# Seven-product up-projection: partial sums added in PSUM banks instead of by VectorE

## The chip, the cores and the metric

The kernel runs on one core of a Trainium2 chip. The metric is the device time of one execution in microseconds (us). Before the change the median of three runs is 2451.78 us (2449.66 to 2457.12).

## The reference

One layer of a hybrid backbone on 2048 latent tokens of width 1024: a token mixer (gated recurrence and gMLP), its output projection, then a gated MLP with a 3x3 depthwise convolution. The change lies in the MLP's first half. Cut to that:

```python
GRID_W = 64; D_FF = 2816
h2 = modulate(rmsnorm(x, norm_ffn), sh2, sc2)          # x: (1, 2048, 1024)
a, g = jnp.split(h2 @ w_up, 2, axis=-1)                # w_up: (1024, 2 * 2816)
g = g.reshape(1, 32, 64, 2816)                         # 32 rows of the grid, 64 wide
gc = depthwise_conv_3x3(g, taps, 'SAME') + conv_b
x = x + g2 * ((a * gelu(gc)) @ w_down)
```

All of it is fp32.

## The kernel before, in words

Every fp32 product is made of three matmuls: an operand is split into a high half in the fast fp32r form (a ScalarE cast) and a low half (the rest, a GpSimd subtraction, in function `split`, lines 131 and 132), and the sum of high x high, high x low and low x high goes into one PSUM bank (`mm3`, line 65 by way of the class `Tensor`).

The up-projection saves multiplications by a Strassen-Winograd scheme with seven products for a two-by-two block product. One **unit** is two channel tiles of 128 channels (f and f+1) by one half of the sequence (`hh`, 1024 tokens). It has a kind: `"g"`, the gate branch that is convolved, or `"a"`, the value branch that is multiplied with the GELU. There are 44 units, 22 in each half of the sequence, and 308 products. A product i has K = 512, four steps of 128, with three 128x512 matmuls each: 12 matmuls into one bank. The scheme's sums of weights (`Unit.prep`) are made by GpSimd, three products ahead of use (`LOOK = 3`); four buffers each hold the high (`Ah`) and low (`Al`) weight tiles. The token side, seven high and seven low tiles `B`, was made before and lies in SBUF.

The list `prods` sets the order: units go in pairs, and the products of the two units of a pair alternate, with the second unit three places behind:

```python
at = first[n] if n < 2 else [14 * (n // 2) + 2 * i + 3 * (n % 2) for i in range(7)]
```

In the middle of each half, a pair is one `"g"` unit and the `"a"` unit of two channel pairs earlier, which by then has its convolved gate; the first pair is `"g"`, `"g"` and the last `"a"`, `"a"`.

Each product gets a bank of its own from `ubank` (four banks in turn). `after(u, i, p)` takes it out. Product 0 is copied to an SBUF tile `keep` by ScalarE (line 1454); products 2 and 3 are added to it by VectorE (1457, 1460); product 4 serves twice, once in a result and once in the running sum (1472 or 1480); products 1, 4, 5 and 6 each end a quarter of the unit's result, by a VectorE addition into the gate tile `gp` (1466), or, for the value branch, by an addition and a multiplication into the tile `cv` (1473 and 1474 on VectorE, or 1476 on VectorE and 1477 on GpSimd).

When a gate unit is done, `conv` runs for each of its two channel tiles as a generator: two of its steps are called behind each product. ScalarE writes the first tap and the bias into two PSUM banks (tag `dn`, line 1382), VectorE adds eight taps (1385), and ScalarE takes the GELU out into `cv` (1399 in the first half, 1404 in the second). The two halves of the sequence share a row border. The first half leaves the last row's unfinished sum in DRAM, and the second half loads it into an SBUF tile `edges` (1373, 1374), adds the three missing taps there (1390, VectorE), takes the GELU (1405, ScalarE) and multiplies it with the value row left by the first half (1406, GpSimd). `put_m` stores finished tiles.

At the start of the stage the last two token tiles of the step before (the second norm, lines 1239 to 1267) are still in work, spread between the first products by `bg_q.slot()`.

A list scheduler that works from estimated durations orders the instructions of each engine when the kernel is built, except where `pin` keeps the program's order. Each engine then runs its list strictly in that order.

Of the kernel before, what the change touches and what calls it, by code (L numbers as in the profile page):

```python
# [9 lines left out]
F32 = mybir.dt.float32  # L10
# [3 lines left out]
AF = mybir.ActivationFunctionType  # L14
ALU = mybir.AluOpType
# [3 lines left out]
P = 128  # L19
# [9 lines left out]
NF = FF // P  # L29
GW = 64  # L30
# [53 lines left out]
def tile_trunk(ctx, tc, x, c, cx, c_ctx, w_ada, b_ada, norm_mix, norm_ffn, w_in, hg_norm, sgu_g, sgu_b,  # L84
               w_sp, b_sp, w_out, w_up, conv_w, conv_b, w_down, norm_final, masks, out):
    nc = tc.nc
    V, S, G, T = nc.vector, nc.scalar, nc.gpsimd, Tensor(nc.tensor)
# [1059 lines left out]
    xah = pb.tile([P, NR, 4, 512], F32R, tag="xah", name="xah", align_bytes=AL)  # L1147
    xal = pb.tile([P, NR - 1, 4, 512], F32R, tag="xal", name="xal", align_bytes=AL)

    def ubank():  # L1150
        return ps2.tile([P, 512], F32, tag="up", name="up", bufs=4)

    def dbank():
        return ps2.tile([P, 2, 512], F32, tag="dn", name="dn", bufs=2)
# [55 lines left out]
        order += [("a", NF // 2 - 2), ("a", NF // 2 - 1)]  # L1210
        units += [Unit(hh, *o, (1, 2) if n % 2 else (3, 0)) for n, o in enumerate(order)]
    prods = []
    first = [(0, 1, 2, 4, 8, 10, 12), (3, 5, 6, 7, 9, 11, 13)]
    for n, u in enumerate(units):
        at = first[n] if n < 2 else [14 * (n // 2) + 2 * i + 3 * (n % 2) for i in range(7)]
        prods += [(at[i], u, i) for i in range(7)]
    prods = [(u, i) for _, u, i in sorted(prods, key=lambda t: t[0])]
    LOOK = 3
    raw_at = {}
# [138 lines left out]
    def g_rows(hh, f, n2):  # L1358

        return view(gp[f % 4], (1 + 2 * n2) * RW + 1, [[4 * RW, 4], [RW, 2], [1, GW]])  # L1360
# [16 lines left out]
    def conv(hh, f, e):  # L1377

        gt = gp[f % 4]
        cp = dbank().rearrange("p a b -> p (a b)")  # L1380
        cr = cp.rearrange("p (r c) -> p r c", c=GW)
        S.activation(cr, gt[:, 0:RH, 0:GW], AF.Identity, bias=cvb[:, f:f + 1], scale=taps[:, f:f + 1])  # L1382
        yield
        for t in range(1, 9):
            V.scalar_tensor_tensor(out=cr, in0=gt[:, t // 3:t // 3 + RH, t % 3:t % 3 + GW],  # L1385
                                   scalar=taps[:, t * NF + f:t * NF + f + 1], in1=cr, op0=ALU.mult, op1=ALU.add)
            yield
        if hh:
            for t in range(6, 9):
                V.scalar_tensor_tensor(out=e[:, 0, :], in0=gt[:, 1, t % 3:t % 3 + GW],  # L1390
                                       scalar=taps[:, t * NF + f:t * NF + f + 1], in1=e[:, 0, :],
                                       op0=ALU.mult, op1=ALU.add)
        tapped.add((hh, f))
        while out_v[0] == 3:
            yield "full"
        out_v[0] += 1
        vt = v_tile()
        if hh == 0:
            pin(S.activation(vt[:, :TH - GW], cp[:, :TH - GW], AF.Gelu))
            S.copy(e[:, 0, :], cp[:, TH - GW:])  # L1400
            S.dma_start(gs_d[f][:, 1, :], e[:, 0, :])
            pin(G.memset(vt[:, TH - GW:TH], 1.0))
        else:
            pin(S.activation(vt[:, GW:], cp, AF.Gelu))  # L1404
            S.activation(e[:, 0, :], e[:, 0, :], AF.Gelu)
            pin(G.tensor_mul(vt[:, :GW], e[:, 0, :], e[:, 1, :]))
        vals[hh, f] = vt
        yield
# [36 lines left out]
    def quad(p, kind):  # L1445
        return p.rearrange("p (j c) -> p j c", c=P) if kind == "a" else p.rearrange("p (j r c) -> p j r c", r=2, c=GW)

    def after(u, i, p):

        hh, f, kind = u.hh, u.f, u.kind  # L1450
        if i == 0:
            t = pf.tile([P, 2 * 512], F32, tag="keep", name="keep", bufs=2)
            u.u, u.u3 = t[:, :512], t[:, 512:]
            S.copy(u.u, p)
            return
        if i == 2:
            V.tensor_add(u.u, p, u.u)
            return
        if i == 3:
            V.tensor_add(u.u3, p, u.u)  # L1460
            return
        c, n2, add = {1: (0, 0, u.u), 4: (1, 1, u.u3), 5: (0, 1, u.u3), 6: (1, 0, u.u)}[i]
        if kind == "g":
            if f >= 4:
                need(tapped, (hh, f + c - 4))
            V.tensor_add(g_rows(hh, f + c, n2), quad(p, kind), quad(add, kind))  # L1466
        else:
            need(vals, (hh, f + c))
            o = v_cols(hh, f + c, n2)
            if i < 5:  # L1470
                if i == 4:
                    V.tensor_add(u.u, p, u.u)
                V.tensor_add(p, p, add)
                V.tensor_mul(o, quad(p, kind), o)
            else:
                V.tensor_add(add, p, add)  # L1476
                G.tensor_mul(o, quad(add, kind), o)
                put_m(hh, f + c)
        if kind == "g" and i == 4:
            V.tensor_add(u.u, p, u.u)  # L1480
        if kind == "g" and i == 6:
            for ff in (f, f + 1):
                if hh == 0:
                    st(gs_d[ff][:, 0, :], gp[ff % 4][:, RH, 1:GW + 1])
                else:
                    ld(gp[ff % 4][:, 0, 1:GW + 1], gs_d[ff][:, 0, :])
                work.append(conv(hh, ff, edge(hh, ff)))
# [33 lines left out]
    for n, (u, i) in enumerate(((2, 4), (2, 6), (1, 4))):  # L1521
# [2 lines left out]
            ld(t, a_src(0, 0, n))  # L1524
            early[n] = t
        raw_at[pos[len(units) - u, i]] = load
    assert max(n for n, (u, i) in enumerate(prods) if i < NR) == NP - 6
    for n, (u, i) in enumerate(prods):
        now[0] = n
        while stores and (stores[0][0] <= n):  # L1530
            stores.pop(0)[1]()
        while back and back[0] <= n:
            back.pop(0)
            out_v[0] -= 1
        p = ubank()
        hi, lo = u.A[i]
        for k in range(4):
            mm3(p, hi[:, k, :], lo[:, k, :], B[i][0][:, k, :], B[i][1][:, k, :], k == 0, k == 3)
            bg_q.slot()
        if n == 11:  # L1540
            bg_q.drain()
        if n == 12:
            edges = px.tile([P, 7, P], F32R, tag="yst", name="edges", bufs=2, align_bytes=AL).bitcast(F32)
            edges = edges[:, :4, :].rearrange("p f (w c) -> p f w c", w=2)
        with tc.issue_after(scaled[-1].ins) if n < 8 else nullcontext():
            after(u, i, p)
        for j in range(7):
            if last_use[j] == n - 4:
                for w in range(2):
                    load_b(1, j, w)  # L1550
        prep(n + LOOK)
# [266 lines left out]
```

## Time and profile before

| | |
|---|---|
| median of three runs | 2451.78 us |
| profiled execution | 2450.25 us, span 2448.4 us |
| granted clock | 0.997 |
| busy: TensorE / VectorE / ScalarE / GpSimd | 99% / 73% / 39% / 36% |
| first and last matmul of the up-projection start | 1171.3 and 2020.0 us |

PE is TensorE, PEld its weight loads, DVE VectorE, ACT ScalarE, POOL GpSimd, SP SyncE (which issues most DMAs). L1385 is line 1385 of the kernel. In the rows of groups the busy time comes first, then the mean duration of one instruction in ns, then the time that the engine sat idle just before the group and what ended that idle time. In rows of a timeline the first number is the start in us from the span's start, the second the duration. A row of waits gives the total, the number of times and the longest. Matmuls overlap one another in the records (389 ns each), so their pace is read from how many start in a stretch.

### The profile page before, as it was taken

What the parts mean: (1) busy time and instruction counts of PE and PEld (TensorE: products, weight loads), DVE (VectorE), ACT (ScalarE), POOL (GpSimd) and SP (SyncE); (2) the same over time, 40 slices, a digit from 0 to 9 for tenths busy, and PEclk for the clock granted to TensorE, in tenths of its full rate; (3) what the DMA queues carried; (4) which work ended last, traced back from release to release, by engine and by line L of the source; (5) the groups of instructions that cost most, each with busy time, mean ns of one, the idle gap of its engine ahead of it and who ended that gap; (6) DMA issues with size and microseconds to landing.
All of it is one profiled execution on the core that took longest, in us unless ns stands there. A gap on an engine that the chain in (4) does not pass through costs nothing.

```text
span 2448.4 us, 32923 instructions
## 1 busy us (share of the span) xinstructions
PE 2414.5 (99%) x11903; PEld 2010.2 (82%) x11903; DVE 1787.9 (73%) x2445; ACT 943.0 (39%) x1614; POOL 871.1 (36%) x795
## 2 busy tenths in 40 slices
PE   8999999999999999999999999999999999999998
PEld 5888888888888888788788888888888888888887
DVE  5867785756776776466698877769999992776875
ACT  3554334333344333354443333333333342332343
POOL 1232110110111122001688788787778870000002
PEclk9999999999999999999999999999999999999999
DMA  8365446564254234768822222562222238834645
GB/s 302 111 206 173 147 130 212 194 223 152 95 185 155 87 104 144 238 212 264 297 84 90 82 91 85 177 241 85 85 93 94 83 102 349 317 126 146 228 151 197
DMA packets 307855, 400.13 MB, mean 163 GB/s; under 512 B 33113, under 2 KB 216161, under 8 KB 304621
## 3 DMA queue, kind: packets, MB, share of 16 engines
q1 hardware_dynamic: 304404, 397.28, 48.1%
q8 instruction: 94, 1.54, 0.3%
q10 hardware_dynamic: 3289, 0.76, 0.1%
q14 instruction: 68, 0.56, 0.1%
HBM read 288.85 MB, written 109.13 MB: 163 GB/s over the span
## 4 chain that ended last, share of the span: by engine, by line
PE 38%; DVE 6%; issue 3%; POOL 2%; ACT 1%; DMA 1%; POOLq 0%; SPq 0%; ACTq 0%; DVEq 0%
PE up L65 24%; PE dn L65 14%; DVE dn L1385 3%; DVE edges L1390 1%; ACT dn L1382 1%; DVE gp L1466 1%; POOL Al L132 1%; DMA yd<-fl 0%; POOL ra L1677 0%; POOL rr L1678 0%; DVE keep L1460 0%; POOL raw L1203 0%; DVE keep L1476 0%; ACT Ah L131 0%; ACT cv L1404 0%
## 5 line engine op out<-in xcount | busy, mean ns | idle before, releaser
L1385 DVE SCALAR_TENSOR_TENSOR dn<-gp,taps,dn 128x1024 f32<-128x1024 f32 x352 | 449.3, 1283 | 21.1 <-ACT dn L1382 17.9
L65 PE MATMUL up<-yf,Ah 128*128 128x512 f32 x1232 | 393.5, 389 | 0.0
L65 PE MATMUL dn<-thl,mhl 128*128 128x512 f32 x1680 | 381.5, 389 | 1.2 <-ACT thl L131 1.2
L132 POOL TENSOR_TENSOR Al<-raw,Ah 128x512 fp32r<-128x512 f32 x264 | 342.5, 1305 | 95.7 <-ACT Ah L131 85.9
L65 PEld LDWEIGHTS dn<-thl,mhl 128*128 128x128 f32 x1680 | 315.0, 188 | 67.7 <-ACT thl L131 2.0
L65 PE MATMUL pj<-xh,whi 128*128 128x512 f32 x896 | 363.2, 406 | 0.0
L65 PE MATMUL pj<-xl,whi 128*128 128x512 f32 x896 | 351.2, 392 | 1.2 <-POOL xl L132 0.6
L65 PE MATMUL pj<-xh,wlo 128*128 128x512 f32 x896 | 350.7, 392 | 1.7 <-DVE wlo L132 1.7
L65 PE MATMUL up<-xah,Al 128*128 128x512 f32 x704 | 275.5, 391 | 4.0 <-POOL Al L132 3.9
L65 PE MATMUL up<-xah,Ah 128*128 128x512 f32 x704 | 274.5, 390 | 0.6 <-ACT Ah L131 0.6
L65 PEld LDWEIGHTS up<-yf,Ah 128*128 128x128 f32 x1232 | 231.2, 188 | 47.9
L131 ACT CAST Ah<-raw 128x512 fp32r<-128x512 f32 x264 | 160.5, 618 | 276.5 <-PE up L65 210.2
L65 PE MATMUL up<-xal,Ah 128*128 128x512 f32 x528 | 205.5, 389 | 0.0
L65 PE MATMUL up<-yf,Al 128*128 128x512 f32 x528 | 205.3, 389 | 0.0
L65 PEld LDWEIGHTS pj<-xh,wlo 128*128 128x128 f32 x896 | 168.3, 188 | 38.0 <-DVE wlo L132 2.4
L65 PEld LDWEIGHTS pj<-xh,whi 128*128 128x128 f32 x896 | 168.6, 188 | 33.2 <-issue 3.5
L65 PEld LDWEIGHTS pj<-xl,whi 128*128 128x128 f32 x896 | 168.8, 188 | 32.3 <-POOL xl L132 1.5
L65 PE MATMUL dn<-wo,o 128*128 128x512 f32 x768 | 182.9, 394 | 2.3 <-ACT o L131 1.8
L588 POOL TENSOR_TENSOR K<-K,tot 128x512 f32<-128x512 f32 x40 | 50.2, 1254 | 343.5 <-PE sc L65 186.6
L65 PEld LDWEIGHTS dn<-wo,o 128*128 128x128 f32 x768 | 142.0, 188 | 32.0 <-ACT o L131 2.2
L65 PEld LDWEIGHTS up<-xah,Al 128*128 128x128 f32 x704 | 132.1, 188 | 36.4 <-POOL Al L132 9.2
L65 PEld LDWEIGHTS up<-xah,Ah 128*128 128x128 f32 x704 | 132.2, 188 | 27.9 <-ACT Ah L131 1.1
(317 smaller groups left out, 3944.2 us busy)
## 6 DMA issues: line engine op xcount, KB each, us to landing
raw<-in_w_up_dram SPq DMA_DIRECT2D x88, 512.0 KB, 4.6
mr<-m SPq DMA_DIRECT2D x85, 512.0 KB, 5.2
raw<-in_w_in_dram SPq DMA_DIRECT2D x68, 512.0 KB, 3.8
sT<-wd SPq DMA_DIRECT2D x88, 256.0 KB, 4.1
raw<-in_w_ada_dram SPq DMA_DIRECT2D x32, 512.0 KB, 3.6
yf<-yd SPq DMA_DIRECT2D x14, 1024.0 KB
m<-cv SPq DMA_DIRECT2D x22, 544.0 KB, 2.7
raw<-in_w_down_dram SPq DMA_DIRECT2D x22, 512.0 KB, 4.1
```

What stands on the lines that cost most here:

```text
L65: return self.engine.matmul(out, lhsT, rhs, **kw)
L131: keep(S.copy(hi, raw))
L132: (eng or G).tensor_sub(lo, raw, hi.bitcast(F32))
L588: e.tensor_mul(view(K2, row * W + o, src), view(K, o, src), view(tot, t0, [[4, n], [ts, 2], [0, B]]))
L1382: S.activation(cr, gt[:, 0:RH, 0:GW], AF.Identity, bias=cvb[:, f:f + 1], scale=taps[:, f:f + 1])
L1385: V.scalar_tensor_tensor(out=cr, in0=gt[:, t // 3:t // 3 + RH, t % 3:t % 3 + GW], scalar=taps[:, t * NF + f:t * NF + f + 1], in1=cr, op0=A ...
L1390: V.scalar_tensor_tensor(out=e[:, 0, :], in0=gt[:, 1, t % 3:t % 3 + GW], scalar=taps[:, t * NF + f:t * NF + f + 1], in1=e[:, 0, :], op0=AL ...
L1466: V.tensor_add(g_rows(hh, f + c, n2), quad(p, kind), quad(add, kind))
```

## The change

- Products 2, 3 and 5 go on accumulating in product 0's bank, and product 6 in product 4's. Products 2 and 3 are copied out by ScalarE in the middle of the accumulation (to the two halves of `keep`), product 5 ends as a plain ScalarE copy (gate) or a VectorE multiplication (value). VectorE's additions for products 2 and 3 and the second use of product 4 are gone.
- The four banks are split in two tags: `ux` for product 0's bank, `uz` for those of products 1 and 4.
- The order in a pair that starts with a gate unit becomes fixed `steps`, so the pair's products no longer reach into the next pair's. The pairs of two value units keep the old order.
- In a product, all eight matmuls with the high weight tile come first, then the four with the low one.
- In the second half, the border row is copied from SBUF into the convolution's PSUM bank, gets its three taps and its GELU there, and only then does the channel's own convolution start in that bank.

```diff
+    def xbank():
+        return ps2.tile([P, 512], F32, tag="ux", name="ux", bufs=2)
+
+    def zbank():
+        return ps2.tile([P, 512], F32, tag="uz", name="uz", bufs=2)
+
     def ubank():
-        return ps2.tile([P, 512], F32, tag="up", name="up", bufs=4)
+        turn[0] += 1
+        return xbank() if turn[0] % 2 else zbank()
...
-    first = [(0, 1, 2, 4, 8, 10, 12), (3, 5, 6, 7, 9, 11, 13)]
+    steps = ((0, 2, 3, 6, 7, 10, 12), (1, 4, 5, 8, 9, 11, 13))
     for n, u in enumerate(units):
-        at = first[n] if n < 2 else [14 * (n // 2) + 2 * i + 3 * (n % 2) for i in range(7)]
-        prods += [(at[i], u, i) for i in range(7)]
+        at = steps[n % 2] if units[n - n % 2].kind == "g" else [2 * i + 3 * (n % 2) for i in range(7)]
+        prods += [(14 * (n // 2) + at[i], u, i) for i in range(7)]
...
         cr = cp.rearrange("p (r c) -> p r c", c=GW)
+        if hh:
+            S.copy(cp[:, :GW], e[:, 0, :])
+            yield
+            for t in range(6, 9):
+                V.scalar_tensor_tensor(out=cp[:, :GW], in0=gt[:, 1, t % 3:t % 3 + GW],
+                                       scalar=taps[:, t * NF + f:t * NF + f + 1], in1=cp[:, :GW],
+                                       op0=ALU.mult, op1=ALU.add)
+            S.activation(e[:, 0, :], cp[:, :GW], AF.Gelu)
+            yield
         S.activation(cr, gt[:, 0:RH, 0:GW], AF.Identity, bias=cvb[:, f:f + 1], scale=taps[:, f:f + 1])
...
-        if hh:
-            for t in range(6, 9):
-                V.scalar_tensor_tensor(out=e[:, 0, :], in0=gt[:, 1, t % 3:t % 3 + GW], ...
...
-            S.activation(e[:, 0, :], e[:, 0, :], AF.Gelu)
...
-            u.u, u.u3 = t[:, :512], t[:, 512:]
-            S.copy(u.u, p)
+            u.u, u.u2 = t[:, :512], t[:, 512:]
+        if i in (0, 2, 3):
+            S.copy(u.u2 if i == 2 else u.u, p)
             return
-        if i == 2:
-            V.tensor_add(u.u, p, u.u)
-            return
-        if i == 3:
-            V.tensor_add(u.u3, p, u.u)
-            return
-        c, n2, add = {1: (0, 0, u.u), 4: (1, 1, u.u3), 5: (0, 1, u.u3), 6: (1, 0, u.u)}[i]
+        c, n2, add = {1: (0, 0, u.u), 4: (1, 1, u.u), 5: (0, 1, None), 6: (1, 0, u.u2)}[i]
         if kind == "g":
             if f >= 4:
                 need(tapped, (hh, f + c - 4))
-            V.tensor_add(g_rows(hh, f + c, n2), quad(p, kind), quad(add, kind))
+            o = g_rows(hh, f + c, n2)
+            if i == 5:
+                S.copy(o, quad(p, kind))
+            else:
+                V.tensor_add(o, quad(p, kind), quad(add, kind))
         else:
             need(vals, (hh, f + c))
             o = v_cols(hh, f + c, n2)
-            if i < 5:
-                if i == 4:
-                    V.tensor_add(u.u, p, u.u)
+            if i == 1:
                 V.tensor_add(p, p, add)
+            if i in (1, 5):
                 V.tensor_mul(o, quad(p, kind), o)
             else:
                 V.tensor_add(add, p, add)
                 G.tensor_mul(o, quad(add, kind), o)
+            if i > 4:
                 put_m(hh, f + c)
-        if kind == "g" and i == 4:
-            V.tensor_add(u.u, p, u.u)
...
-        p = ubank()
+        if i == 0:
+            u.x = xbank()
+        elif i == 4:
+            u.z = zbank()
+        p = zbank() if i == 1 else u.z if i in (4, 6) else u.x
         hi, lo = u.A[i]
-        for k in range(4):
-            mm3(p, hi[:, k, :], lo[:, k, :], B[i][0][:, k, :], B[i][1][:, k, :], k == 0, k == 3)
-            bg_q.slot()
+        order = [(k, 0, t) for k in range(4) for t in range(2)] + [(k, 1, 0) for k in range(4)]
+        for m, (k, w, t) in enumerate(order):
+            T.matmul(p, (hi, lo)[w][:, k, :], B[i][t][:, k, :], start=(m == 0 and i in (0, 1, 4)),
+                     stop=(m == len(order) - 1), skip_group_check=True)
+            if m % 3 == 2:
+                bg_q.slot()
```

More of the change, by code (lines that the diff above doesn't have):

```diff
@@ L1148, in tile_trunk @@
     xal = pb.tile([P, NR - 1, 4, 512], F32R, tag="xal", name="xal", align_bytes=AL)
+    turn = [0]
+    def xbank():
+        return ps2.tile([P, 512], F32, tag="ux", name="ux", bufs=2)
+    def zbank():
+        return ps2.tile([P, 512], F32, tag="uz", name="uz", bufs=2)
     def ubank():
-        return ps2.tile([P, 512], F32, tag="up", name="up", bufs=4)
+        turn[0] += 1
+        return xbank() if turn[0] % 2 else zbank()
     def dbank():
@@ L1387, in conv @@
             yield
-        if hh:
-            for t in range(6, 9):
-                V.scalar_tensor_tensor(out=e[:, 0, :], in0=gt[:, 1, t % 3:t % 3 + GW],
-                                       scalar=taps[:, t * NF + f:t * NF + f + 1], in1=e[:, 0, :],
-                                       op0=ALU.mult, op1=ALU.add)
         tapped.add((hh, f))
@@ L1526, in tile_trunk @@
         raw_at[pos[len(units) - u, i]] = load
-    assert max(n for n, (u, i) in enumerate(prods) if i < NR) == NP - 6
     for n, (u, i) in enumerate(prods):
```

## The prediction, made before the changed kernel ran

> **What bounds the kernel now.** The page is read first: busy time per engine and the costliest groups. Then the stage that the change touches, the up-projection from 1171 to 2020 us, is cut into four stretches, and the waits and groups inside it are read.
>
> ```profile
> PE 2414.5 (99%) x11903; PEld 2010.2 (82%) x11903; DVE 1787.9 (73%) x2445; ACT 943.0 (39%) x1614; POOL 871.1 (36%) x795
> ```
> ```profile
> 1171.00:1231.00 60.00, 58.48 (x263) 46.77 (x261) 43.39 (x62) 27.06 (x46) 41.03 (x32) 1.00 0.81 270
> 1231.00:1598.00 367.00, 366.82 (x1619) 303.63 (x1618) 298.01 (x322) 136.78 (x216) 294.29 (x253) 1.00 0.33 108
> 1598.00:1800.00 202.00, 200.07 (x881) 164.84 (x880) 180.66 (x204) 72.72 (x116) 161.43 (x136) 1.00 0.36 125
> 1800.00:2020.00 220.00, 218.81 (x958) 179.20 (x958) 204.10 (x220) 83.00 (x128) 172.79 (x147) 1.00 0.28 93
> sum 849.00, PE 844.17 PEld 694.44 DVE 726.16 ACT 319.56 POOL 669.54; mean PE 211.04 PEld 173.61 DVE 181.54 ACT 79.89 POOL 167.39
> ```
> The columns are the stretch, its length, busy time and count of PE, PEld, DVE, ACT and POOL, the granted clock, DMA share and GB/s TensorE is the bound, at full clock, and the change leaves its matmuls alone: 12 of 128x512 a product, 308 products. The second stretch has no idle time worth the name, so it gives the pace: 367.00/1619 = 0.2267 us a matmul, 2.72 us a product. By that pace the third stretch needs 881 x 0.2267 = 199.7 and lost 2.3 us, the fourth needs 217.2 and lost 2.8.
>
> ```profile
> L69 PE MATMUL dn<-ident,cv 128*128 128x128 f32 x16 | 2.6, 275 | 0.3 <-DVE cv L1239 0.3
> L69 PE MATMUL up<-ident,cv 128*128 128x128 f32 x4 | 0.6, 271 | 0.0
> ```
> The first stretch holds 20 transposes (3.2 us); its other 243 matmuls need 55.1, so it lost 1.7 us. Together 6.8 us, or 0.28% of the kernel: that is all that this stage can give, whatever is taken from VectorE. The stretch just behind it lost 80 - 346 x 0.2267 = 1.6 us more:
>
> ```profile
> 2020.00:2100.00 80.00, 78.83 (x346) 64.49 (x345) 30.94 (x36) 24.11 (x34) 2.91 (x2) 1.00 0.89 340
> ```
>
> ```profile
> PE up L65 <- POOL Al L132: 3.9, 7, 1.4
> PE up L65 <- ACT Ah L131: 0.6, 1, 0.6
> ```
> These are TensorE's waits in the stage (us in total, times, longest): not for a bank or for VectorE, but for the low half of a weight tile, Al, that GpSimd subtracts. The lost time is larger than 4.5 us, since matmuls are pipelined and each wait also costs a restart. Why Al is late differs: at the start the queues are full of the second norm, in the second half VectorE is behind, and ScalarE, which makes the high halves in order, stands behind it:
>
> ```profile
> ACT edges L1405 <- DVE edges L1390: 70.9, 20, 5.3
> ACT dn L1382 <- DVE gp L1466: 34.5, 16, 4.8
> ACT Ah L131 <- POOL fl L1199: 29.7, 11, 5.6
> ```
> The first of these exists only in the second half of the sequence. VectorE there is 204.10/220 = 93% busy.
>
> **The change, part by part.** VectorE's share:
>
> ```profile
> L1457 DVE TENSOR_TENSOR keep<-up,keep 128x512 f32<-128x512 f32 x44 | 30.2, 687 | 38.7 <-PE up L65 37.8 <-POOL raw L1197 0.8
> L1385 DVE SCALAR_TENSOR_TENSOR dn<-gp,taps,dn 128x1024 f32<-128x1024 f32 x352 | 449.3, 1283 | 21.1 <-ACT dn L1382 17.9
> L1390 DVE SCALAR_TENSOR_TENSOR edges<-gp,taps,edges x66: 271/1068/1398, 1610.2 to 1985.9; 128x64 f32<-128x64 f32 x66
> ```
> Each unit loses four of its 0.687 us adds: those of products 2 and 3, the second add of product 4, and in gate units the add of product 5, in value units the separate add into the bank at product 4. That is 44 x 4 x 0.687 = 121 us. The 66 edge taps of 64 elements take from 0.271 to 1.398 us (minimum, median, maximum). Their spread comes without any larger work, and GpSimd is busy nearly all the time; the taps that work in PSUM (1.283 us for 1024 elements) have no such excess. An edge tap in PSUM is bounded by the 0.271 of the fastest and the 1.068 of the median; I take 0.271, since the shape is the same and the PSUM tap rows look unhindered. That saves 66 x 0.68 = 45 us by the mean of 0.955 (62.8 us in the group row below) and nothing by the other end. The Trainium skill, "SBUF — State Buffer", section "Who interferes with whom", says that a VectorE instruction with both inputs in SBUF blocks against a GpSimd instruction reading SBUF, and that one with a single SBUF input does not; the trace's spread agrees, and by that rule the low price holds.
>
> ```profile
> L1390 DVE SCALAR_TENSOR_TENSOR edges<-gp,taps,edges 128x64 f32<-128x64 f32 x66 | 62.8, 955 | 0.7
> ```
> VectorE in the stage goes from 726 to about 560 us, 66%. None of that is TensorE's time; it counts only through ScalarE, which no longer stands 5 us behind an edge tap.
>
> ScalarE gets the copies:
>
> ```profile
> L1454 ACT COPY keep<-up 128x512 f32<-128x512 f32 x44 | 25.7, 584 | 12.3 <-POOL cv L1477 12.3
> L1400 ACT COPY edges<-dn 128x64 f32<-128x64 f32 x22 | 4.4, 202 | 0.0
> L131 ACT CAST Ah<-raw 128x512 fp32r<-128x512 f32 x262 | 159.3, 618 | 276.5 <-PE up L65 210.2 <-POOL Al L132 38.0 <-issue 16.0
> ```
> Products 2 and 3 of 44 units and product 5 of 22 gate units: 110 x 0.584 = 64.2 us, and 22 edge copies of 0.2 us, 4.4. ScalarE goes from 320 to 388 of 849 us, 46%, and covers it: it idles 276 us ahead of the casts of Ah. If that cover were gone, a copy would delay the next cast by 0.58 us, against a lead of three products, 8.2 us. GpSimd's work is the same count (the value unit's multiply of product 4 takes the place of that of product 5). On SyncE the weight loads tied to product 4 are issued one or two products earlier, those tied to product 6 as before, and the stores of a value unit two products earlier: 0, or a little sooner free buffers.
>
> The new wait: product 2 may not start in product 0's bank before ScalarE has copied it out, nor 3 before the copy of 2, nor 5 before that of 3; 6 waits for VectorE's read of 4. Behind TensorE's waiting matmul stands every later product of both units. In a middle pair the order is g0 a0 g1 g2 a1 a2 g3 g4 a3 a4 g5 a5 g6 a6, so at least two products, 5.44 us, lie between a product and the next one in its bank. A copy starting up to 4.86 us late costs nothing. In the steady stretch the copy follows its product at once:
>
> ```profile
> 1405.26 0.62 ACT L131 CAST Ah<-s 128x512 fp32r<-128x512 f32 x1 [2.13 <-PE up L65]
> 1405.79 0.58 ACT L1454 COPY keep<-up 128x512 f32<-128x512 f32 x1
> ```
> Both were released by products around 1405, and nothing is late. So the second stretch stays as it is, 0. Two places are tighter. In the last pair of each half the old staggered order stays, with one product (2.72 us) between products 2 and 3: a copy may start 2.1 us late. Most will fit; four such places at 0 to 1 us: I take +0.5. And the start:
>
> ```profile
> 1183.03 0.39 PE L65 MATMUL up<-xah,Al 128*128 128x512 f32 x1
> 1183.26 0.39 PE L65 MATMUL up<-xah,Ah 128*128 128x512 f32 x1
> ...
> 1190.09 1.02 ACT L1252 ACTIVATE fl<-dn,s,a 128x256 f32<-128x256 f32 x2 [3.21 <-POOL Al L132]
> 1191.00 0.58 ACT L1454 COPY keep<-up 128x512 f32<-128x512 f32 x1
> ```
> The second unit's first product ended at 1183.4, and its copy began 7.6 us later, behind a norm activation that waited for GpSimd. A copy of product 2 in that place would end at 1191.6; the first unit's product 3 is the seventh product and wants its bank at about 1171.3 (the first start in the row below) + 6 x 2.72 + 1.9 (12 transposes at 2.6/16) = 1189.5: a wait of 2.1 us. The second unit's products 1 and 2 also come one product earlier than now, and their weights are the ones whose Al ended at 1190.05:
>
> ```profile
> L65 PE MATMUL up<-xah,Ah x704: 387/389/478, 1171.3 to 2006.0; 128*128 128x512 f32 x176
> ```
> ```profile
> 1188.77 1.28 POOL L132 TENSOR_TENSOR Al<-fl,Ah 128x512 fp32r<-128x512 f32 x1
> ```
> Against that stands the order of high parts first: Al is wanted eight matmuls, 1.81 us, later. That is more than the longest Al wait of the table, 1.4. Start: between -1.7 (all its loss goes) and +4 (2.1 and as much as 1.9 for the weights); I take +1.
>
> In the third and fourth stretches the 1.81 us alone cover every Al wait, and the lighter VectorE removes the cause. Of 2.3 and 2.8 I take 1.9 and 2.4; what is late next there is nothing by the waits table except one wait for Ah of 0.6, which stays.
>
> The edge row moves ahead of the convolution: a copy of 0.20, three taps of 0.27, a GELU of 0.26 (the row is below) lengthen a channel's chain from 1.21 + 8 x 1.28 + 1.02 = 12.5 to some 13.8 us, with two channels per pair of units, 14 products or 38.1 us; the 10.5 us that are left hide it. Its two loads on SyncE are wanted before the first tap and no longer after the eighth; they land in 1.5 us and are issued when the unit's last product is emitted, so ScalarE's copy could wait about 2 us once a channel, which the lead of three products covers.
>
> ```profile
> L1405 ACT ACTIVATE edges<-edges 128x64 f32<-128x64 f32 x22 | 5.7, 258 | 70.9 <-DVE edges L1390 70.9
> L1382 ACT ACTIVATE dn<-gp,vec,taps 128x1024 f32<-128x1024 f32 x44 | 53.3, 1211 | 41.8 <-DVE gp L1466 34.5 <-ACT edges L1400 4.1 <-issue 2.9
> L1404 ACT ACTIVATE cv<-dn 128x1024 f32<-128x1024 f32 x22 | 22.5, 1022 | 12.7 <-DVE dn L1385 10.4 <-DMA m<-cv 2.3
> DMA to landing us min/median/max: 1.5/1.5/1.7
> ```
> The sum: +1 + 0 - 1.9 - 2.4 + 0.5 = -2.8 us. The profiled execution took 2450.25 us, 1.5 under the median of the three runs (2451.78, from 2449.66 to 2457.12). Taken off the median it gives 2449.0 us.
>
> **The rivals.** First, slower: ScalarE's copies become what TensorE waits for, at the banks of products 0, 2 and 3. It decides from a copy that starts 4.86 us after its product. For it: ScalarE's longest waits now are 4.8, 5.3 and 5.6 us, and it works in order. Against it: the 5.3 belongs to the edge taps that get cheap, and the steady stretch shows no late copy. Should one copy a pair start behind a 5.6 us wait, it would end about 6.2 us after its product, 0.74 us too late; over 22 pairs that is 16 us, less the 4 gained: 2464. At one such wait in a unit it is 2480. The Trainium skill, "Perfetto Trace Analysis", section "Matmuls", advises that independent groups rotate through banks so that the copy-out of one overlaps the next group's matmuls; the change holds a bank over four products, and this rival is what that rule would make of it. Chance 0.23.
>
> Second, faster by over 0.3%: everything lost goes, start and the stretch behind included, 6.8 + 1.6 = 8.4 us: 2443.4. For it, the 1.81 us; against it, the start. Chance 0.20.
>
> Third, nothing moves: Al is late because raw weights and GpSimd are late, so waits shift by as much as they shrink, and TensorE ends within 1 us: 2451.8. For it, GpSimd is 80% busy and the first seven preparations of a pair now hold two subtractions each in a row. Against it, in the second stretch that density gives no wait. Chance 0.15. The forecast itself has 0.42.
>
> **How the numbers follow.** The bound for no change is 0.3%, 7.4 us, about what a measurement of this kernel can tell. The forecast and the third rival lie within it, 0.57, less 0.02 for a start that goes badly; the second gives 0.20 faster, the first 0.25 slower with that 0.02. The range runs from 2442, the whole loss gone and a little of the runs' spread, up to 2462, short of the first rival with one wait a pair; outside lie about 2 in 10.
>
> **What would show it.** Right: no TensorE wait for Al in the table, VectorE near 560 us and ScalarE near 388 in the stage, edge taps at 0.27 us, the stage 3 to 5 us shorter from 1598 on, and a wait of TensorE for a ScalarE copy (keep) in the first 60 us alone. Wrong: waits of TensorE for keep or gp copies that repeat once a pair, or edge taps still near 1 us, or a pace that differs from 0.2267 us.

## The result, and the profile after

The changed kernel takes 2445.29 us (median of 8 runs, 2442.25 to 2446.63) against 2451.45 us (8 runs, 2448.36 to 2457.12). The ratio is 0.9972, with a 95% interval from 0.9961 to 0.9983: 6 to 7 us faster, clear of noise, and just short of 0.3%. The profiled execution took 2444.85 us, its span 2443.1 us.

First the page's busy times, then the same stretches of the stage as before (length, busy time and count of PE, PEld, DVE, ACT, POOL, clock, DMA share, GB/s).

```profile
PE 2413.3 (99%) x11903; PEld 2011.3 (82%) x11903; DVE 1645.2 (67%) x2269; ACT 1009.6 (41%) x1746; POOL 872.3 (36%) x795
```
```profile
1171.00:1231.00 60.00, 58.75 (x266) 47.53 (x265) 39.50 (x52) 31.77 (x54) 46.40 (x37) 1.00 0.79 265
1231.00:1598.00 367.00, 367.00 (x1620) 303.87 (x1619) 253.54 (x242) 161.77 (x264) 295.17 (x254) 1.00 0.33 111
1598.00:1800.00 202.00, 202.00 (x893) 167.26 (x892) 141.51 (x165) 93.14 (x160) 165.78 (x141) 1.00 0.34 121
1800.00:2020.00 220.00, 219.90 (x970) 181.76 (x969) 152.43 (x173) 99.23 (x162) 169.81 (x142) 1.00 0.29 99
sum 849.00, PE 847.65 PEld 700.41 DVE 586.98 ACT 385.91 POOL 677.17; mean PE 211.91 PEld 175.10 DVE 146.75 ACT 96.48 POOL 169.29
```

The matmuls, their count and their pace in the second stretch are the same (367.00/1620 = 0.2265 us). But the third stretch now holds 893 of them in place of 881, and the fourth 970 in place of 958 (the last up-projection matmul now starts at 2014.2 us, so the fourth also holds some of the next stage): TensorE is never idle there. VectorE lost 139 us in the stage and ScalarE gained 66.

TensorE's waits in the stage, all of them; then the edge taps (minimum, median, maximum in ns); then the groups that answer to those shown of before:

```profile
PE ux L65 <- POOL Al L132: 1.2, 2, 0.6
```
```profile
L1395 DVE SCALAR_TENSOR_TENSOR dn<-gp,taps,dn x66: 277/286/291, 1631.7 to 1986.7; 128x64 f32<-128x64 f32 x66
```
```profile
L1467 ACT COPY keep<-ux 128x512 f32<-128x512 f32 x132 | 77.1, 584 | 19.0 <-PE ux L65 18.1 <-POOL cv L1487 0.6 <-DVE gp L1477 0.3
...
L1475 ACT COPY gp<-ux 128x512 f32<-128x512 f32 x22 | 13.1, 594 | 11.5 <-PE ux L65 11.4
L1398 ACT ACTIVATE edges<-dn 128x64 f32<-128x64 f32 x22 | 4.9, 224 | 12.8 <-DVE dn L1395 12.7
```

The edge taps (now L1395) have lost their spread: 277 to 291 ns, where 271 to 1398 stood. ScalarE's wait for edge taps fell from 70.9 us to 12.7.

A sharper measure for what follows is the **lost time of the stage**: over all its matmuls in order of start, the part of each step from one start to the next that exceeds the steady pace (0.2266 us; 0.109 behind a transpose), steps within 8 ns of it left out. Before it is 9.5 us: 3.9 up to 1233 us (the start), nothing to about 1597, 3.8 to about 1806 (the border of the two halves and what follows), 1.8 behind that (a wait in every pair of units). After it is 2.7, all of it at the start, mostly 0.3 at 1189.5 us behind a `keep` copy and two waits for Al, at 1223.6 and 1229.9 us, of 0.9 each with the restart. That is 6.7 us less; the rest of the kernel behind the stage took 0.5 us more (428.9 against 428.4 us from the last up-projection matmul's start to the end). The two make the measured difference. The start of the stage itself scatters: two executions of the changed kernel reached it at 1172.3 and 1175.2 us with 2.7 and 2.8 us lost in it, so single spans are not compared below.

### The profile page after: what moved, and what is told of

Same layout as the page of the kernel before. It is cut to its first block, busy times and chain, and to the rows that moved or that the text cites. A ratio compares the mean times of both kernels' runs of the same rounds, so it can differ in the third digit from the quotient of the medians.

```text
span 2443.1 us, 32683 instructions
## 1 busy us (share of the span) xinstructions
PE 2413.3 (99%) x11903; PEld 2011.3 (82%) x11903; DVE 1645.2 (67%) x2269; ACT 1009.6 (41%) x1746; POOL 872.3 (36%) x795
## 4 chain that ended last, share of the span: by engine, by line
PE 55%; issue 2%; POOL 1%; DVE 1%; ACT 1%; DMA 0%; POOLq 0%; SPq 0%; ACTq 0%
PE dn L65 21%; PE ux L65 19%; PE uz L65 14%; PE pj L65 0%; DMA raw<-oT 0%; POOL ra L1692 0%; PE ux L69 0%; POOL rr L1693 0%; PE uz L69 0%; POOL Al L132 0%; DVE dn L1403 0%; ACT mhl L131 0%; ACT jk L1684 0%; DVE odd L80 0%; ACT odd L1762 0%
## 5 line engine op out<-in xcount | busy, mean ns | idle before, releaser
L65 PE MATMUL ux<-xah,Ah 128*128 128x512 f32 x528 | 205.7, 390 | 0.0
L65 PE MATMUL uz<-yf,Ah 128*128 128x512 f32 x704 | 174.0, 389 | 0.0
L65 PE MATMUL ux<-yf,Ah 128*128 128x512 f32 x528 | 155.4, 389 | 0.0
L65 PEld LDWEIGHTS uz<-yf,Ah 128*128 128x128 f32 x704 | 132.1, 188 | 27.4
L65 PE MATMUL ux<-xah,Al 128*128 128x512 f32 x528 | 141.7, 390 | 1.2 <-POOL Al L132 1.2
L132 DVE TENSOR_TENSOR wlo<-raw,whi 128x1024 fp32r<-128x1024 f32 x68 | 84.9, 1249 | 83.9 <-ACT whi L131 78.1
L65 PE MATMUL ux<-xal,Ah 128*128 128x512 f32 x352 | 137.0, 389 | 0.0
L1692 POOL TENSOR_SCALAR ra<-ss 128x1 f32<-128x1 f32 x8 | 5.3, 662 | 360.4 <-ACT jk L1684 360.4
```

Of the source, the lines that this page charges most:

```text
L65: return self.engine.matmul(out, lhsT, rhs, **kw)
L132: (eng or G).tensor_sub(lo, raw, hi.bitcast(F32))
L1692: G.tensor_scalar(out=a, in0=ss, scalar1=plus, scalar2=None, op0=ALU.add)
```

## The experiments

The change has three parts that can be had alone: **A**, the additions in PSUM with the order of products that they need; **B**, the border row in PSUM; **C**, high parts first. All combinations were run. The columns of the table are the ratio to the kernel before (95% interval), the lost time of the stage in its four parts, and VectorE's busy time between 1800 and 2000 us, as a share. The parts are stretches of time and not single places: "border" is all that is lost between 1597 and 1806 us.

| parts | ratio | start | first half | border | recurring | sum | VectorE |
|---|---|---|---|---|---|---|---|
| none | 1 | 3.9 | 0.0 | 3.8 | 1.8 | 9.5 | 92% |
| C | 0.9988 (0.9979 to 0.9998) | 2.8 | 0 | 0.3 | 5.7 | 8.8 | 89% |
| B | 1.0014 (1.0006 to 1.0023) | 4.0 | 0.0 | 3.5 | 0 | 7.6 | 82% |
| A | 0.9998 (0.9989 to 1.0006) | 5.6 | 0 | 3.0 | 0 | 8.6 | 80% |
| B, C | 0.9991 (0.9983 to 1.0000) | 3.1 | 0 | 2.6 | 0 | 5.7 | 82% |
| A, B | 0.9991 (0.9982 to 0.9999) | 5.0 | 0 | 1.6 | 0 | 6.7 | 68% |
| A, C | 0.9977 (0.9969 to 0.9986) | 3.2 | 0 | 0.8 | 0 | 4.0 | 79% |
| A, B, C | 0.9972 (0.9961 to 0.9983) | 2.7 | 0 | 0 | 0 | 2.7 | 71% |

**C alone.** On the kernel before:

```diff
-            mm3(p, hi[:, k, :], lo[:, k, :], B[i][0][:, k, :], B[i][1][:, k, :], k == 0, k == 3)
+        order = [(k, 0, t) for k in range(4) for t in range(2)] + [(k, 1, 0) for k in range(4)]
+        for m, (k, w, t) in enumerate(order): ...
```

> The kernel before with one part of the change alone: in each product the eight matmuls with the high weight tile come first, then the four with the low one. Theory A (the low tiles are only a little late; 1.81 us more for them cover every wait): TensorE's waits for Al go from 3.9 us to under 0.5, the up-projection loses about 2 us instead of the 7 to 9 of before, time 4 to 6 us less, as much as the whole change. Theory B (in the second half VectorE's work for a pair of units takes a little longer than TensorE's, so lateness builds up whatever is tolerated): the waits are put off, not removed; the late ones of the second half (0.3 us a pair) come back after the 1.81 us are used up, 2 to 3 us less. Theory C (VectorE's load alone matters): under 1 us less.

TensorE's waits in the stage:

```profile
PE up L65 <- DVE cv L1474: 3.1, 5, 0.6
PE up L65 <- ACT keep L1454: 0.8, 1, 0.8
PE dn L69 <- DVE cv L1239: 0.4, 1, 0.4
```

The waits for Al are gone entirely, as theory A has it, and the border with them. But TensorE now waits once a pair for a bank that VectorE has yet to read (L1474), with 0.8 us lost and another 0.2 a little later, and the second half is worse than before. VectorE is busy for 89% of a stretch in which TensorE waits for it:

```profile
1800.00:2000.00 200.00, 196.81 (x858) 160.03 (x857) 177.24 (x195) 73.03 (x117) 158.26 (x136) 1.00 0.28 89
```

That is theory B: the late engine is VectorE, and a later demand for Al only changes where TensorE meets it. VectorE's own waits in the same 200 us say so too. Before, and with C alone, it waits for ScalarE's first tap of a convolution and never for TensorE; in the changed kernel it waits for TensorE's products seven times (the first row is of before, the second of C alone; they are all of VectorE's waits there; the last two are the changed kernel's waits for TensorE):

```profile
DVE dn L1385 <- ACT dn L1382: 13.3, 6, 2.4
DVE dn L1385 <- ACT dn L1382: 21.9, 11, 2.9
DVE gp L1477 <- PE uz L65: 9.5, 4, 2.4
DVE keep L1486 <- PE uz L65: 5.7, 3, 1.9
```

In all six kernels that have A or B, VectorE waits for TensorE there, for 12 to 29 us. The measured 2.9 us of gain by the ratio are more than the 0.7 of this one trace.

**B alone.** On the kernel before, the `if hh:` block of the diff above:

> The kernel before with the border row's three taps and GELU moved into the convolution's PSUM bank, ahead of the channel's own taps; nothing else. The 66 edge taps should go from a mean of 0.955 us to about 0.29, VectorE 44 us less in the second half, and ScalarE's 70.9 us behind edge taps to under 15. Theory A: the waits for Al in the first half of the sequence and at its end (1216 to 1231 and 1611 us) stay, those from 1772 us on go, 3 us less. Theory B: the same, since VectorE falls below TensorE's pace in the second half, 3 us less, and with it no wait for Al after 1650 us. Theory C: 1 to 2 us less, as the additions from PSUM are the larger part of VectorE's load (121 against 45 us).

The recurring waits go, as expected by A and B alike. The start stays; at the border the long wait for Al near 1612 us stays, and a new wait of 1.8 us, for a bank that VectorE has yet to read, comes at 1655 us. Yet the kernel is slower, by 2.0 us by the medians and 3.4 by the ratio. The loss is behind the stage, where the down-projection takes over the banks (waits from 2010 us on):

```profile
PE dn L65 <- DVE keep L1479: 3.1, 2, 2.4
PE dn L65 <- ACT thl L131: 1.2, 2, 0.7
```

VectorE was still at the last value unit; just before, it had itself stood 3.3 us for a GELU of ScalarE, 0.9 us in the kernel before. From the stage's last start to the end it takes 433.7 us in place of 428.4. No theory had this loss.

**The change without C.** On the changed kernel:

```diff
-        order = [(k, 0, t) for k in range(4) for t in range(2)] + [(k, 1, 0) for k in range(4)]
+        order = [(k, w, t) for k in range(4) for w, t in ((0, 0), (0, 1), (1, 0))]
```

> The changed kernel with the old order of matmuls in a product (high x high, high x low, low x high for each step of K). Theory A: waits for Al come back, 2 to 5 us more than the changed kernel, mostly in the first 60 us of the stage and at the border of the two halves. Theory B: only the first 60 us and the border suffer, the second half stays free of waits because VectorE is at 70%: 1.5 to 3 us more. Theory C: no difference, within 1 us.

```profile
PE ux L65 <- POOL Al L132: 5.0, 4, 1.7
```

Four waits for Al, three at the start and one at the border, none recurring; the lost time is 3.9 us larger, and the time 4.7 us by the ratios. The places fit both theories, as A put the waits mostly there; the size lies in A's range (2 to 5) and above B's (1.5 to 3). This run alone does not decide between them.

**The change without B.** The edge taps and their GELU go back to where they were:

> The changed kernel with the border row's taps back in SBUF, after the channel's eight taps, and its GELU at the end. Edge taps back near 1 us, VectorE 45 us more, ScalarE behind edge taps again, by some 40 to 70 us. Theory A: no TensorE wait comes back, since Al has 1.81 us more: within 1 us of the changed kernel. Theory B: the same, because VectorE stays under TensorE's pace (about 80%). Rival D (ScalarE, which now copies the banks of products 0, 2 and 3 and works in order, is held up by 3 to 5 us behind an edge tap, and TensorE waits for the bank): waits of TensorE for keep copies, about 0.5 to 1 us a pair in the second half, 5 to 10 us more.

ScalarE stands behind edge taps for 20.9 us (the expectation was 40 to 70), and TensorE waits 0.5 us once for a `keep` copy; the lost time is 1.3 us larger. Beside A and C, the border row's move is worth 1 us, within the intervals.

**B and C, without A:**

> The kernel before with high parts first and the border row in PSUM, but with VectorE's additions of products as they were: the change without its main part. If the lighter VectorE matters only by falling under TensorE's pace in the second half (theory B), the two small parts are enough inside the stage: lost time there 3 to 4 us as in the changed kernel (2.7), though the end of the stage may wait 3 to 5 us for VectorE as it did with the border row alone; 2449 to 2451. If the additions in PSUM are what counts (theory C), waits for banks stay in the second half as with high parts first alone, some 0.8 us a pair, lost 7 to 8, 2451 to 2453.

```profile
PE up L65 <- DVE gp L1469: 2.3, 1, 2.3
PE up L65 <- ACT keep L1457: 0.8, 1, 0.8
PE dn L69 <- DVE cv L1239: 0.4, 1, 0.4
PE up L65 <- ACT Ah L131: 0.2, 1, 0.2
```

No recurring wait, as theory B has it; but at the border VectorE holds a bank for 2.3 us, and behind the stage another 0.8 us go (1.1 with the restart). The lost time of 5.7 lies between what theories B (3 to 4) and C (7 to 8) expected.

**A alone:**

> The changed kernel with the old order of matmuls in a product and the border row in SBUF: the additions in PSUM and the new order of products alone. Theory B: VectorE is at some 77%, the second half has no wait a pair; the starts of both halves wait for Al as without high parts first (lost 6 to 8): 2449 to 2451. Theory C: the additions alone bring the whole gain, lost under 4, 2446. Rival D: with ScalarE held up behind edge taps, TensorE waits for keep copies, 0.5 us a pair, lost over 9, 2453.

```profile
PE ux L65 <- POOL Al L132: 6.0, 5, 1.9
PE ux L65 <- ACT keep L1464: 0.4, 1, 0.4
```

The largest part of the change gains nothing alone that can be measured, though it takes VectorE from 92% to 80% in the second half. It ends the recurring waits, and with its order of products and the old order of matmuls the start is worse by 1.7 us.

**One product between copy and next use.** The old staggered order in all pairs but the very first:

```diff
-        at = steps[n % 2] if units[n - n % 2].kind == "g" else [2 * i + 3 * (n % 2) for i in range(7)]
+        at = steps[n % 2] if n < 2 else [2 * i + 3 * (n % 2) for i in range(7)]
```

> The changed kernel with the old staggered order in all pairs but the very first, so that one product and not two lies between products 2 and 3 of a unit (2.72 us instead of 5.44). If ScalarE's copies start within 2.1 us of their product, as in the steady stretch, nothing is lost there, lost 3 to 5 in the stage, 2446 to 2448. If copies are later than that once a pair (behind the cast that waits for GpSimd's sum), 0.5 to 2 us a pair are lost, mostly as waits for keep: 10 to 40 us more than the changed kernel.

```profile
PE ux L65 <- ACT keep L1467: 1.7, 3, 1.1
PE uz L65 <- ACT Ah L131: 0.5, 1, 0.5
```

The ratio is 0.9981 (0.9973 to 0.9990), 2.2 us more than the changed kernel by the ratios, and the lost time 4.5 us (3 to 5 were expected), of which TensorE's waits for copies make 1.7 us in three places and nothing recurs. Copies do start within 2.1 us of their product in nearly every pair (123 of 132 copies).

**No product between.** Products 2 and 3 of a unit directly behind each other:

```diff
-    steps = ((0, 2, 3, 6, 7, 10, 12), (1, 4, 5, 8, 9, 11, 13))
+    steps = ((0, 2, 3, 4, 8, 10, 12), (1, 5, 6, 7, 9, 11, 13))
```

> The changed kernel with products 2 and 3 of a unit following each other directly, in all pairs that start with a gate unit: each of these 40 copies is exposed. It prices the rival in which TensorE waits for the copy-out. At least 0.6 us (a copy) plus handing over, 0.9 in sum, less nothing: 40 x 0.9 = 36 us more; if ScalarE is held up as well, 2 us each, 80 us more; if a pause is followed by matmuls at a lower clock, more still. Less than 20 us more would say that copies overlap the next product in a way that I do not see.

```profile
PE ux L65 <- ACT keep L1467: 31.7, 19, 5.4
PE ux L65 <- POOL Al L132: 0.3, 1, 0.3
```

The ratio is 1.0151 (1.0137 to 1.0165), 36 us more than before. The price is near the lower expectation (40 x 0.9 = 36 us), but by luck, since it comes another way: in a middle pair the scheduler moved matmuls of another product (four of them, 0.91 us, in the pair at 1320 us) into the gaps. There one copy follows its product at once and is hidden; the other starts 1.9 us after its product, behind a convolution's first tap and a weight cast of ScalarE. Such a copy costs 1.3 to 1.6 us of lost time in most pairs; three places cost 3.6 to 5.7 us, each with a spell of slow matmuls behind it (last section).

**VectorE loaded again.** The changed kernel, with copies that nothing reads:

```diff
             V.scalar_tensor_tensor(out=cr, in0=gt[:, t // 3:t // 3 + RH, t % 3:t % 3 + GW], ...
+            if hh:
+                V.tensor_copy(junk, cp[:, :512])
```

> The changed kernel with work added on VectorE alone: behind each of the eight taps of a channel in the second half of the sequence, it also copies half of the convolution's bank (128x512) into an SBUF tile that nothing reads. That is 176 copies of some 0.6 to 0.7 us, 110 to 120 us, which takes VectorE from 70% to about 97% in the second half; TensorE waits for none of it directly. Theory B (VectorE at TensorE's pace is what matters): waits return once a pair in the second half though high parts come first, about 0.3 to 1 us a pair, 4 to 12 us in all and none in the first half. Theory A (1.81 us for Al cover it): within 1 us of the changed kernel.

TensorE's waits in the stage up to 2030 us (it ends at 2086), what ScalarE waited for from 1640 to 2050 us, and TensorE's waits from 2080 us on:

```profile
PE ux L65 <- ACT keep L1470: 34.1, 15, 4.2
PE ux L65 <- POOL Al L132: 1.7, 2, 1.1
PE ux L65 <- ACT Ah L131: 0.3, 1, 0.3
```
```profile
ACT keep L1470 <- POOL cv L1490: 47.4, 9, 7.6
...
ACT cv L1420 <- DVE junk L1407: 7.8, 9, 1.5
```
```profile
PE dn L65 <- ACT cv L1420: 29.7, 2, 19.7
PE uz L65 <- DVE keep L1489: 2.0, 2, 1.2
```

The ratio is 1.0390 (1.0376 to 1.0404): 94 us more than before, 100 more than the changed kernel, for at most 120 us of work on an engine that TensorE doesn't wait for directly. Nothing is lost in the first half behind its start; 65 us are lost in the second, and 35 more behind the stage. Theory B was right in kind, and its size (4 to 12 us) was far too small. The way that the lateness takes to TensorE is the prediction's first rival at work. In one pair of units (VectorE, ScalarE, GpSimd, ScalarE):

```profile
1851.01 0.68 DVE L1489 TENSOR_TENSOR keep<-uz,keep 128x512 f32<-128x512 f32 x1
1856.43 1.03 ACT L1420 ACTIVATE cv<-dn 128x1024 f32<-128x1024 f32 x1 [0.39 <-DVE junk L1407]
1862.71 2.49 POOL L1490 TENSOR_TENSOR cv<-keep,cv 128x512 f32<-128x512 f32 x2
1865.24 0.59 ACT L1470 COPY keep<-ux 128x512 f32<-128x512 f32 x1 [4.59 <-POOL cv L1490]
```

VectorE's two adds into `keep` are done at 1844.3 and 1851.7 us. But GpSimd's multiplies also need the GELU of the value unit's gate, and VectorE has only just finished its taps and copies for it: the GELU ends at 1857.5 us, where in the middle pairs of the changed kernel it ends some 17 us ahead of the adds. Another 5 us pass because GpSimd's list has weight sums and an Al ahead of the two multiplies. Until they are done `keep` is not free, ScalarE's copy stands (up to 7.6 us), and TensorE waits for the bank. So a late VectorE and the order of GpSimd's list both have a part in the price, and they were not taken apart. VectorE itself is busy for only 81% between 1800 and 2000 us: its work for a pair is 36.3 us, 95% of the 38.1 us that a pair took before, but the pair now takes 45. A share of busy time tells of lateness only where TensorE isn't held up.

**Low halves ahead of sums on GpSimd**, for the two waits that the changed kernel has left:

```diff
-            split(hi, lo, (a11, a12, self.s2, a11, a21, a12, a22)[i])
+            split(hi, lo, (a11, a12, self.s2, a11, a21, a12, a22)[i], keep=pin if i == 2 else lambda t: t)
...
-                G.tensor_add(a11, self.s2, a11)
+                pin(G.tensor_add(a11, self.s2, a11))
```

> The changed kernel with one order fixed on GpSimd: at product 2 of a unit the low half Al is subtracted before the next two sums of weights, which the scheduler had put ahead of it. The two waits for Al that are left in the changed kernel (0.8 us each, at 1223.6 and 1229.9 us) were for such tiles, made 2.6 us after their sum was ready. Expected: both go, lost in the stage from 2.7 to about 1.2, 1.5 us less than the changed kernel. The price could be that GpSimd stands idle for ScalarE's cast (0.7 us, twice a pair), at 80% busy: if that is too much, waits for Al appear once a pair, 0.5 us each, 10 us more.

Both waits for Al are gone, and the ratio is 0.9999 (0.9990 to 1.0008): the gain of the whole change is lost. ScalarE in the second half, by its timeline:

```profile
1644.23 0.59 ACT L1467 COPY keep<-ux 128x512 f32<-128x512 f32 x1 [4.85 <-PE ux L65]
1651.32 1.02 ACT L1417 ACTIVATE cv<-dn 128x1024 f32<-128x1024 f32 x1 [6.50 <-DVE dn L1403]
1652.24 0.61 ACT L131 CAST Ah<-fl 128x512 fp32r<-128x512 f32 x1
1652.75 1.14 ACT L131 CAST Ah<-raw 128x512 fp32r<-128x512 f32 x2
```

Here a GELU came into ScalarE's list ahead of three weight casts and waited 6.5 us for VectorE's taps; TensorE then waited 6.0 us for Ah. In the changed kernel the first of these casts runs at 1641.1 us and the GELU at 1652.5. Two orders fixed on GpSimd, in every unit, had moved the scheduler's list of another engine, at one place some 420 us behind the two waits that were meant.

**The same for the second pair of units alone:**

> The changed kernel with Al subtracted before the next sum of weights on GpSimd for the units of the second pair of the first half alone, the third and fourth units, where the two waits of 0.8 us stand; everywhere else the scheduler's order stays, so the 6 us wait in the second half that came with the fixed order in all units should not come. Expected: one or both waits gone, lost in the stage 1.2 to 2.5 in place of 2.7 to 2.8, 0.3 to 1.5 us less than the changed kernel, too little for the times to show: a ratio to the kernel before of 0.996 to 0.998. If fixing an order anywhere moves the scheduler's order elsewhere, a wait of several us can come up at another place.

The ratio is 0.9964 (0.9950 to 0.9977), the lost time 2.4 us: the waits for Al went, one for Ah of 1.0 us came. The changed kernel was also run again, beside the loaded VectorE and the fixed order in all units:

> The changed kernel once more, on the same chip as the two others of this call: 2445 to 2447, lost in the stage 2.7, so that the two can be compared with it.

It has 0.9973 (0.9964 to 0.9982) and a lost time of 2.8 us. The two can't be told apart.

How well does the ledger of lost time explain the times? Lost time plus the time behind the stage, against the kernel before, gives -6.3 us for the change (measured -6.2 by the medians), -0.1 for A (-0.4), -2.4 for A and B (-2.5), -5.1 for A and C (-6.4), +3.4 for B (+2.0), -2.8 for B and C (-1.9), -4.5 for one product between (-4.0), +37.3 for no product between (+36.4) and +94.7 for the loaded VectorE (+94.4). It fails by 1.6 to 3.4 us for C (-0.7 against -2.3), for the fixed GpSimd order (+2.1 against -0.7) and for that order in the second pair alone (-6.6 against -10.0, five runs), where one trace may not stand for all executions.

## Why the prediction was right, and where not

It named the direction and the cause of the gain, and the time fell in its range, which was 20 us wide; but it forecast 2.8 us and 6 to 7 came. The 2445.3 us lie nearer to its second rival (2443.4, everything lost goes, chance 0.20) than to the forecast (2449.0, chance 0.42). Point by point:

- *TensorE is the bound, and only its lost time can be gained.* Right, and this kept the forecast small: VectorE lost 139 us, and the kernel 6. The bound of 6.8 us for the stage was too low, though: by the starts of the matmuls 9.5 us were lost before. Most of the difference is in the first stretch, which was said to lose 1.7: its transposes were charged with 3.2 us of recorded time, but they start 0.11 us apart and overlap.
- *The start, +1.* This is the term that was mis-sized: it measured -1.1 (3.9 to 2.7). The wait for a late copy that it priced at 2.1 us was there, behind the same norm activation, but the copy began at 1189.28 and not at 1191.0, and the lost time at that place is 0.3 us with the restart (0.6 in the second trace). The weights of the second unit were made in time, with the 1.81 us of high parts first: without them A makes the start worse, to 5.0 and 5.6, as the step feared.

```profile
1188.36 1.02 ACT L1261 ACTIVATE fl<-dn,s,a 128x256 f32<-128x256 f32 x2 [2.98 <-POOL Al L132]
1189.28 0.58 ACT L1467 COPY keep<-ux 128x512 f32<-128x512 f32 x1
```

- *Third and fourth stretch, -1.9 and -2.4.* All of the 2.3 and 2.8 went (5.6 together by the starts). I had kept back 0.8, for the one wait for Ah of 0.6, which went as well, and +0.5 for the tight places in the last pairs, where nothing was lost. Those two, 1.3 us, and the start's 2.1 are most of the 3.9 us between the forecast and the stage's gain of 6.7.
- *"The 1.81 us alone cover every Al wait."* True of Al and wrong of the time: with C alone the waits for Al are gone, but the second half loses more than before, at VectorE's banks. Among the eight kernels of the table the recurring waits stay only in the two where VectorE is busy for 89 to 92% and never waits for TensorE, and go in all with 82% or less. The gain there needs the lighter VectorE, and at the start and the border it needs the later Al; neither part alone has the whole. At the start even both leave two waits for Al.
- *Edge taps at 0.271 us.* 0.286. The spread of 277 to 291 ns against 271 to 1398 comes with one SBUF input less. In the four kernels of the table with the row in SBUF, the 25 taps that ran while GpSimd was idle took 270 to 287 ns, and all slower ones ran beside a GpSimd instruction; with the row in PSUM, 56 of the changed kernel's 66 ran beside one and were no slower. That agrees with the Trainium skill, "SBUF — State Buffer", section "Who interferes with whom", which the prediction cited.
- *VectorE to 560 us.* 587. The adds are recorded at 0.68 us but start 0.60 apart, so that 176 of them are 106 us of busy time and not 121. The rest is overlap too: counted from each start to the next one, the 352 taps that stay take 436 us where they took 428, as fewer instructions follow directly behind them.

```profile
1230.04 0.68 DVE L1473 TENSOR_TENSOR up<-up,keep 128x512 f32<-128x512 f32 x1
1230.64 0.68 DVE L1457 TENSOR_TENSOR keep<-up,keep 128x512 f32<-128x512 f32 x1
```

- *The rival, copies late.* It did not happen in the changed kernel, with two products between: behind the first 30 us of the stage its copies start up to 3.2 us after their product in most pairs, and 4.7 to 4.8 us after it in two, within the 4.86 us that cost nothing. Its price was shown by taking the products away (1.3 to 1.6 us a pair) and by loading VectorE (about 6 us of lost time a pair in the second half). So holding a bank over several products, against the advice of the Trainium skill ("Perfetto Trace Analysis", section "Matmuls") as the prediction read it, costs nothing here as long as the copies come within the products between.
- *The signs.* Of those named for being right, ScalarE came near 388 us (386), the stage from 1598 us on was shorter (by 5.6 us and not 3 to 5), no wait for a copy repeats, and the one loss behind a copy lies in the first 60 us. Two waits for Al are left, against the sign "no TensorE wait for Al".

What stays open: why C alone makes the recurring waits larger (1.8 to 5.7) and not merely other, and how much of the loaded kernel's loss is VectorE's lateness and how much GpSimd's order. The order of every engine's list changes with the edit, and that was not taken apart.

## What to carry to other kernels

Where TensorE is busy for 99%, first add up what it loses per stage and to whom: that is all that an edit elsewhere can give, and taking 139 us from another engine may be worth 6. A wait names the last link, not the late engine: making the named operand wanted later moves the wait to the next thing that the late engine owes, so ask which engine is at the pace of the bound, and whether it ever waits for the bound. And with lists that a scheduler orders, an order fixed in every unit can cost more at one of them, on another engine, than it gains where it was meant: read all waits of the new trace, not those of the place.

## What the runs showed of the hardware

A pause of TensorE can cost more than its length. With the border row alone, two waits of 0.66 and 2.44 us behind the stage were followed by matmuls that start 0.43 us apart in place of 0.227, nine of them, and the granted clock of that stretch is 0.66:

```profile
2021.42 0.40 PE L65 MATMUL dn<-Ah,mhl 128*128 128x512 f32 x1
2024.26 0.64 PE L65 MATMUL dn<-Ah,mhl 128*128 128x512 f32 x1 [2.44 <-DVE keep L1479]
2024.69 0.63 PE L65 MATMUL dn<-Al,mhl 128*128 128x512 f32 x1
```
```profile
2024.00:2029.00 5.00, 4.74 (x14) 3.78 (x15) 0.20 (x1) 0.00 (x0) 1.28 (x1) 0.66 0.76 267
```

The wait of 2.29 us in the kernel with B and C has a clock of 1.00 behind it; behind one of 2.42 us in the loaded kernel (at 2071.5 us) and those of 1.3 to 1.4 us with no product between, the matmuls keep their pace. All waits from 2.95 to 6 us in the stage had slow spells behind them. The Trainium skill, "TensorE: Matmul & The Clock Gate", section "What's actually happening", has the clock halved after an idle window of about 3.4 us, in windows that run free of the program; here less idle time was enough (0.66 and 2.44 us, 3.1 together, within 4.1 us), and the halving agrees nearly (0.43 against 0.227).
